# HGRN's state over chunks of 128 tokens, and mLSTM's gate chain in steps between projections

## The chip, the cores and the metric

The kernel runs on one core of one Trainium2 chip. The metric is the device time of one execution in microseconds (us), as the median of the runs given; lower is better.

## The reference, cut to what matters

The program is a two-layer transformer block followed by a second two-layer block. The change touches one stage of the second block, `mixer_ab`: over 256 context and 512 latent tokens it runs HGRN with four heads of 128 x 128 state and mLSTM with four heads, each forward and backward. All of it is float32.

```
def hgrn2_chunk_scan(q, k, v, logf, state0):      # CHUNK = 32
    def step(S, xs):
        b = jnp.cumsum(fc, axis=1)
        b_mid = b[:, CHUNK // 2 - 1:CHUNK // 2]
        b_last = b[:, -1:]
        A = jnp.einsum('bthd,bshd->bhts', qc * jnp.exp(b - b_mid), kc * jnp.exp(b_mid - b))
        A = jnp.where(mask, A, 0.0)
        o = (jnp.einsum('bhts,bshe->bthe', A, vc)
             + jnp.einsum('bthd,bhde->bthe', qc * jnp.exp(b), S))
        S_new = (S * jnp.exp(b_last[:, 0])[..., None]
                 + jnp.einsum('bshd,bshe->bhde', kc * jnp.exp(b_last - b), vc))

def mlstm_chunk_scan(q, k, v, ig, logf, state0):  # its gates alone
        D = jnp.where(mask, bh[..., :, None] - bh[..., None, :] + igh[..., None, :], -jnp.inf)
        m_inter = bh + m[..., None]
        m_t = jnp.maximum(D.max(-1), m_inter)
```

A chunk's tokens act on each other through the matrix A, and on later chunks through the state S. The length of a chunk is free: the decays exp(b) multiply along the tokens, so the same result comes out of longer chunks if A also holds the products between what used to be separate chunks.

## The kernel before

TensorE's order is the order of the code; a scheduler sets the order of the other engines when the kernel is built. All 768 tokens stand side by side in the free dimension. A projection (`proj2`, `mm2`) multiplies one 128-column block of the weights with eight blocks of the normed input; each product of float32 is made of three passes over operands split in two (`hh`/`hl`, `whi`/`wlo`). One of its eight steps is six matmuls on line 1019: three over 512 columns and three over 258. VectorE (DVE) reads the result out of PSUM (`scaled`, L1033 to L1036), ScalarE (ACT) adds biases and splits the weights' high part (L306), GpSimd (POOL) makes the low part in this stage (L307).

Between those steps stands side work. `later` puts a generator at the end of a list, and after each step `tick` advances the first generator of the list by one `yield`. So what a generator issues up to its next `yield` comes on TensorE between two steps of a projection, and if its operands are late, TensorE stands still in front of it, with the projections behind.

`mixer_ab` goes through it in this order:

- the gates' projection and then the whole gate chain of mLSTM (L1088 to L1151): bias, log-sigmoid, two scans over 768 tokens for each direction (L1115, called twice), a running maximum, exponentials, two stores to DRAM (`dm`). `by_token` (L1153 to L1160) transposes two of its results to tokens on partitions; `later` gives it a delay of 16 steps.
- four HGRN heads. `hgrn_in(h)` makes the projections z forward, z backward, q and v, and from z the scan of log decays (L1220), the factors `al`, and the scaled k and q (q by POOL, L1244). `hgrn_core(h)` is a generator with 29 yields: it transposes v to tokens (`tokens`, L1053) and copies it to a block-diagonal `vblk` by four 32-partition copies (L1254), transposes k for both directions, makes A for 128 tokens at a time and keeps the 32 x 32 diagonal blocks by a predicated copy under a mask (L1269, L1271), scales q by `al` on POOL (L1278 to L1281), and then walks through 6 blocks of 128 tokens and 4 chunks of 32 in each. For a block: A times v (L1297), and one product of 512 columns of k with `vblk` that gives the four chunks' state updates side by side (L1302). For a chunk: 32 columns of q times the state (L1313), and the next state by one DVE instruction (L1321), for both directions, then `yield`.
- `conv` and `values` projections, and four mLSTM heads (`mlstm_head`) as generators, the gates' projections, `finish`.

Of the kernel before, what the change touches and what calls it, by code (L numbers as in the profile page):

```python
# [17 lines left out]
P = 128  # L18
# [241 lines left out]
class Body:  # L260
# [800 lines left out]
    def mixer_ab(self, r):  # L1061
# [23 lines left out]
        b = self.small(2)  # L1085
        nc.vector.tensor_scalar(b, ps[:, 0, SC:SC + 2], c2("gb", 0), None, ALU.add)
# [3 lines left out]
        ig, fg = T(), T()  # L1090
        self.both(lambda c, s: nc.vector.tensor_scalar(ig[G, c], tg[G, c], b[G, s:s + 1], None, ALU.add))
        self.both(lambda c, s: nc.vector.tensor_scalar(fg[G, c], tg[H, c], b[H, s:s + 1], None, ALU.add))
        ig, fg = ig[G, :T2], fg[G, :T2]
        ab = T()[G, :T2]
        nc.vector.scalar_tensor_tensor(ab, fg, -1.0, fg, ALU.mult, ALU.max)
        self.log_exp()
        nc.scalar.activation(ab, ab, AF.Exp, scale=-1.0)
        nc.scalar.activation(ab, ab, AF.Ln, bias=self.ones[G, 0:1])
        nc.vector.scalar_tensor_tensor(fg, fg, 0.0, ab, ALU.min, ALU.subtract)
        bc = T()[G, :T2]  # L1100
# [6 lines left out]
        rm, rx = resets(P, 0.0, 1.0), resets(P, -1e30, 0.0)  # L1107
        ch = lambda t, n=P: t.rearrange("p (c n) -> p c n", n=n)

        def scan(out, mask, x, init, op0, op1):  # L1110

            for d in range(2):
                q = slice(32 * d, 32 * d + 32)
                st = (1, -1)[d]
                nc.vector.tensor_tensor_scan(out[q, ::st], mask[q], x[q, ::st], init, op0, op1)  # L1115

        scan(bc, rm, fg, 0.0, ALU.mult, ALU.add)
        aw = T()[:, :T2]
        a = aw[G]
        nc.vector.tensor_tensor(a, ig, bc, ALU.subtract)  # L1120
        cm = T()[G, :T2]
        scan(cm, rx, a, -1e30, ALU.add, ALU.max)

        so = self.ar.tile([P, 12], F32, tag="so", name="so")
        mp = so[:, 6:12]
        nc.vector.tensor_tensor_scan(so[0:32, 0:6], cm[0:32, 127::P], bc[0:32, 127::P], 0.0, ALU.max, ALU.add)
        nc.vector.tensor_tensor_scan(so[32:64, 1::-1], cm[32:64, P::-P], bc[32:64, P::-P], 0.0, ALU.max, ALU.add)
        nc.vector.tensor_tensor_scan(so[32:64, 5:1:-1], cm[32:64, 5 * P:P:-P], bc[32:64, 5 * P:P:-P],
                                     so[32:64, 0:1], ALU.max, ALU.add)
        nc.vector.memset(mp[G], 0.0)  # L1130
        nc.vector.tensor_copy(mp[0:32, 1:6], so[0:32, 0:5])
        nc.vector.tensor_copy(mp[32:64, 0:1], so[32:64, 1:2])
        nc.vector.tensor_copy(mp[32:64, 5:6], so[32:64, 0:1])
        nc.vector.tensor_copy(mp[32:64, 2:5], so[32:64, 3:6])
        mpb = mp[G].unsqueeze(2).to_broadcast([64, 6, P])
        nc.vector.tensor_tensor(ch(cm), ch(cm), mpb, ALU.max)
        dm = self.dr.tile([2, 64, T2], F32, tag="dm", name="dm")
        nc.sync.dma_start(dm[0], cm)
        wi = T()[G, :T2]
        nc.vector.tensor_tensor(ch(wi), mpb, ch(cm), ALU.subtract)  # L1140
        nc.scalar.activation(wi, wi, AF.Exp)
        nc.sync.dma_start(dm[1], wi)
        em = bc
        nc.vector.tensor_tensor(em, bc, cm, ALU.add)
        nc.scalar.activation(em, em, AF.Exp, scale=-1.0)
        wk = T()[G, :T2]
        for n, o in ((0, 127), (32, 0)):
            q = slice(n, n + 32)
            nc.vector.tensor_tensor(ch(wk)[q], ch(a)[q], ch(cm)[q, :, o:o + 1].to_broadcast([32, 6, P]), ALU.subtract)
        nc.scalar.activation(aw[H], wk, AF.Exp)  # L1150
        awc = T()[:, :T2].rearrange("p (t e) -> p t e", e=P)  # L1151
        emc = self.ar.tile([P, 6, 64], F32, tag="emc", name="emc")

        def by_token():
            self.tokens(awc, aw, "v")
            pt = self.aux()
            for t in range(6):
                nc.tensor.transpose(pt[:, t * 64:(t + 1) * 64], em[:, t * P:(t + 1) * P], self.ident[G, 0:64])
            nc.vector.tensor_copy(emc, pt[:, :384].rearrange("p (t e) -> p t e", e=64))
            yield  # L1160

        self.later(by_token(), 16)
# [31 lines left out]
        vblk = self.ar.tile([P, 6, 4, P], F32, tag="vblk", name="vblk")  # L1194
        nc.gpsimd.memset(vblk, 0.0)

        def hgrn_in(h):
            z, zb = [], []
            for d in range(2):
                t = T()  # L1200
                zb.append(self.scaled(t, self.proj2(self.SEG, ("hg", h), d), r))
                z.append(t)
            sg, sn = [], []
# [10 lines left out]
            for d in range(2):  # L1214
# [7 lines left out]
                b3 = ch(bb, 32)  # L1222
# [20 lines left out]
            for d in range(2):  # L1243
                nc.gpsimd.tensor_tensor(res[d][0], res[d][0], q[:, :T2], ALU.mult)  # L1244
# [752 lines left out]
```

## Time and profile before

| what | us |
| --- | --- |
| median of 3 runs (3003.11 to 3011.44) | 3007.16 |
| the profiled execution, its own time | 3008.77 |
| its span in the profile | 3007.0 |
| TensorE (PE) busy | 2888.8 (96%) |
| DVE busy | 1884.5 (63%) |
| ACT busy | 1190.7 (40%) |
| POOL busy | 555.3 (18%) |

The stage of the change lies between 1208 us and about 1695 us of the span. Times in the rows are microseconds from the start of the span unless marked ns. A matmul of full float32 operands shows as two records; those of the projections and transposes show as one. Matmul ends are modelled, so the length of a piece of work on PE is read here from the start of its first record to the start of the next row. A bracket at the end of a row gives the idle time before it and what ended it.

### The profile page before, as it was taken

The numbers are of one execution on the slowest core, as the hardware profiler recorded it, in microseconds if no ns is written. First come the engines' busy times: TensorE is split into PE (matmuls) and PEld (weight loads), VectorE is DVE, ScalarE is ACT, GpSimd is POOL, SyncE is SP. The second block draws the span as 40 slices with busy tenths as digits, with TensorE's granted clock in tenths as the row PEclk, the third lists the DMA queues.
The fourth block names the chain that finished last, engine by engine and source line by source line (L and its number), as shares of the span: only waits on it lengthen the run. The fifth ranks groups of instructions, "written<-read, shape, count | busy, mean of one in ns | idle before, by whom it ended". The sixth has DMA issues, their size and how long they took to land. (4 is left out here: it accounts for less than half of the span.)

```text
span 3007.0 us, 42444 instructions
## 1 busy us (share of the span) xinstructions
PE 2888.8 (96%) x16570; PEld 2466.9 (82%) x16570; DVE 1884.5 (63%) x3608; ACT 1190.7 (40%) x2081; POOL 555.3 (18%) x434
## 2 busy tenths in 40 slices
PE   9999999999999999899999989999999899999997
PEld 7777888877788888766767888888889788899997
DVE  7679995567699976755544563433444779545445
ACT  5663222347542224432334553121123678532223
POOL 3630000046300002423333140000001420300002
PEclk9999999999999999999999999999999999999999
DMA  4235663331266642210121301222222210233332
GB/s 147 69 104 174 200 198 98 89 114 54 70 195 198 197 154 95 69 36 29 36 74 53 106 25 61 63 64 64 64 63 64 78 43 15 95 95 92 96 95 71
DMA packets 98936, 278.47 MB, mean 93 GB/s; under 512 B 11504, under 2 KB 16880, under 8 KB 98224
## 3 DMA queue, kind: packets, MB, share of 16 engines
q1 hardware_dynamic: 98736, 275.76, 29.3%
q8 instruction: 130, 2.13, 0.3%
q14 instruction: 70, 0.57, 0.1%
HBM read 264.84 MB, written 6.68 MB: 90 GB/s over the span
## 5 line engine op out<-in xcount | busy, mean ns | idle before, releaser
L306 ACT ACTIVATE whi<-raw 128x1024 fp32r<-128x1024 f32 (+1 forms) x363 | 377.9, 1042 | 1279.8 <-PE b L1019 468.9
L1019 PE MATMUL b<-hh,whi 128*128 128x512 f32 (+1 forms) x2000 | 655.4, 328 | 0.0
L1019 PE MATMUL b<-hh,wlo 128*128 128x258 f32 x2000 | 475.3, 319 | 0.0
L1019 PE MATMUL b<-hl,whi 128*128 128x512 f32 (+1 forms) x2000 | 469.1, 316 | 0.0
L307 DVE TENSOR_TENSOR wlo<-raw,whi 128x1024 fp32r<-128x1024 f32 (+1 forms) x321 | 391.6, 1220 | 99.1 <-ACT whi L306 97.1
L1019 PEld LDWEIGHTS b<-hh,whi 128*128 128x128 f32 x2000 | 378.9, 189 | 52.5 <-issue 23.1
L1019 PEld LDWEIGHTS b<-hl,whi 128*128 128x128 f32 x2000 | 348.4, 189 | 48.7 <-issue 1.2
L1019 PEld LDWEIGHTS b<-hh,wlo 128*128 128x128 f32 x2000 | 313.9, 191 | 0.0
L334 PE MATMUL b<-hbl,whi 128*128 128x512 f32 x704 | 275.3, 391 | 2.6 <-DVE hbl L345 2.6
L333 PE MATMUL b<-hbh,whi 128*128 128x512 f32 x704 | 275.8, 392 | 1.1 <-ACT hbh L344 1.1
L869 DVE SCALAR_TENSOR_TENSOR junk<-araw,cond 128x512 f32<-128x512 f32 x384 | 271.6, 707 | 7.6 <-ACT cond L355 2.0
L335 PE MATMUL b<-hbh,wlo 128*128 128x512 f32 x704 | 275.1, 391 | 0.2 <-DVE wlo L307 0.2
L1555 POOL TENSOR_TENSOR acc<-acc,t 128x256 f32<-128x256 f32 (+1 forms) x54 | 48.9, 906 | 1011.6 <-ACT t L1550 1010.8
L1019 PE MATMUL b<-t,whi 128*128 128x512 f32 (+1 forms) x864 | 212.5, 354 | 0.0
L392 POOL TENSOR_TENSOR acc<-acc,sq 128x512 f32<-128x512 f32 (+1 forms) x33 | 47.5, 1438 | 761.5 <-ACT sq L389 760.9
L1019 PEld LDWEIGHTS b<-t,whi 128*128 128x128 f32 x864 | 162.3, 188 | 29.8
L334 PEld LDWEIGHTS b<-hbl,whi 128*128 128x128 f32 x704 | 132.8, 189 | 31.4 <-DVE hbl L345 3.3
L333 PEld LDWEIGHTS b<-hbh,whi 128*128 128x128 f32 x704 | 132.7, 189 | 29.5 <-ACT hbh L344 1.5
L335 PEld LDWEIGHTS b<-hbh,wlo 128*128 128x128 f32 x704 | 132.8, 189 | 28.5 <-DVE wlo L307 1.0
L307 POOL TENSOR_TENSOR wlo<-raw,whi 128x1024 fp32r<-128x1024 f32 x42 | 105.7, 2519 | 251.7 <-ACT whi L306 193.0
L335 PE MATMUL b<-hidh,wlo 128*128 128x512 f32 (+1 forms) x352 | 134.1, 381 | 1.1 <-DVE wlo L307 1.1
L333 PE MATMUL b<-hidh,whi 128*128 128x512 f32 (+1 forms) x352 | 133.7, 380 | 0.0
(445 smaller groups left out, 5766.8 us busy)
## 6 DMA issues: line engine op xcount, KB each, us to landing
raw<-w SPq DMA_DIRECT2D x365, 512.0 KB, 3.5
araw<-ada SPq DMA_DIRECT2D x192, 256.0 KB, 3.0
raw<-w SPq DMA_DIRECT2D x18, 256.0 KB, 2.7
xr<-xd SPq DMA_DIRECT2D x2, 2048.0 KB, 8.2
t<-dm SPq DMA_DIRECT2D x8, 384.0 KB, 5.7
x<-xT SPq DMA_DIRECT2D x8, 256.0 KB, 5.2
kTh<-krh SPq DMA_DIRECT2D x32, 64.0 KB, 2.0
kTl<-krl SPq DMA_DIRECT2D x32, 64.0 KB, 2.0
```

What stands on the lines that cost most here:

```text
L306: self.last = nc.scalar.activation(hi[:, :m], r, AF.Copy).ins
L307: self.lo_eng.tensor_tensor(lo[:, :m], r, hi[:, :m].bitcast(F32), ALU.subtract)
L333: t.matmul(out, ah, bh, start=start, stop=False, skip_group_check=True)
L334: t.matmul(out, ah, bl, start=False, stop=False, skip_group_check=True)
L335: t.matmul(out, al, bh, start=False, stop=stop, skip_group_check=True)
L392: nc.gpsimd.tensor_tensor(acc[:, c], acc[:, c], t[:, c], ALU.add)
L869: nc.vector.scalar_tensor_tensor(junk, raw, 1.0, self.cond[:, s, k], ALU.mult, ALU.mult, accum_out=self.adah[:, i, t, s:s + 1])
L1019: t.matmul(ps[:, b, :w_], w[:, s], x[:, o:o + w_], start=(k == 0 and b not in seen), stop=(k == n - 1 and i == 2), skip_group_check=True)
L1555: nc.gpsimd.tensor_tensor(ac, ac, t, ALU.add)
```

## The change

HGRN's state goes over chunks of 128 tokens: six updates for a head and direction in place of 24. The products between the four 32-token chunks of a block, which went through the state before, now go into A in two further levels. At each level k and q are first scaled so that their decays meet at a common point. `hgrn_in` makes 66 decay factors for a direction (`fa`) where it made 24 (`al`).

- Level 1 (L1284 to L1289) makes A as before; DVE then scales half of k (128x12x32).
- Level 2 (L1301 to L1306) multiplies, for each direction, 12 pairs of 32 x 32 tokens, copies them to A with four small DVE copies, scales all of k on DVE (L1305) and all of q on POOL (L1306).
- Level 3 (L1316 to L1323) multiplies 6 pairs of 64 x 64 tokens, copies them to A on ACT, and scales half of k on DVE and half of q on POOL (L1323).
- The transposes of k come after that. The state then takes one product of 128 columns for the update (L1348) and one of all 128 tokens of a block with the state (L1350), and one DVE instruction (L1357), with one `yield` for a block. `vblk`, its memset and its copies are gone.

The gate chain becomes a generator of its own with six yields. `hgrn_in` advances it after the projections z, z and q of heads 1 and 2; what is left would run behind head 2. `by_token` goes to the list behind head 2's core. The arena has 34 tiles in place of 30.

```diff
+        gb = self.small(2)
+        nc.vector.tensor_scalar(gb, ps[:, 0, SC:SC + 2], c2("gb", 0), None, ALU.add)
...
+        def gate_chain():
...
+            ig, fg = T(), T()
+            self.both(lambda c, s: nc.vector.tensor_scalar(ig[G, c], tg[G, c], gb[G, s:s + 1], None, ALU.add))
...
+            nc.vector.scalar_tensor_tensor(ab, fg, -1.0, fg, ALU.mult, ALU.max)
             yield
...
+            self.log_exp()
...
+            scan(bc, rm, fg, 0.0, ALU.mult, ALU.add)
+            yield
...
+            scan(cm, rx, a, -1e30, ALU.add, ALU.max)
+            yield
...
+            nc.sync.dma_start(dm[0], cm)
+            yield
...
+            nc.scalar.activation(em, em, AF.Exp, scale=-1.0)
+            yield
...
+            nc.scalar.activation(aw[H], wk, AF.Exp)
+            yield
...
-        self.later(by_token(), 16)
+            self.later(by_token(), 0)
...
+        chain = gate_chain()
...
-        vblk = self.ar.tile([P, 6, 4, P], F32, tag="vblk", name="vblk")
-        nc.gpsimd.memset(vblk, 0.0)
...
+                if h:
+                    next(chain, None)
...
+                fi, se = (0, 1)[::(1, -1)[d]]
+                b3, b4 = ch(bb, 32), bb.rearrange("p (m i n) -> p m i n", i=2, n=32)
+                fa = self.ar.tile([P, 66], F32, tag="fa", bufs=4, name=self.nm("fa"))
+                lm = self.ar.tile([P, 12, 2], F32, tag="lm", bufs=2, name=self.nm("lm"))
+                f1, gk, hv, dec = fa[:, 0:12], fa[:, 12:24], fa[:, 48:60], fa[:, 60:66]
+                qh = fa[:, 24:48].rearrange("p (m i) -> p m i", i=2)
+                nc.vector.tensor_tensor(lm, b4[:, :, :, last], b4[:, :, :, mid], ALU.subtract)
+                nc.vector.tensor_tensor(f1, lm[:, :, fi], b4[:, :, se, mid], ALU.add)
+                nc.vector.tensor_copy(gk, lm[:, :, se])
+                nc.vector.tensor_copy(qh[:, :, fi], b4[:, :, fi, mid])
+                nc.vector.tensor_tensor(qh[:, :, se], b4[:, :, se, mid], b4[:, :, fi, last], ALU.add)
+                nc.vector.tensor_tensor(hv, b4[:, :, 0, last], b4[:, :, 1, last], ALU.add)
+                nc.vector.tensor_tensor(dec, hv[:, ::2], hv[:, 1::2], ALU.add)
+                nc.scalar.activation(fa, fa, AF.Exp)
...
-            for c in range(4):
-                s = slice(32 * c, 32 * c + 32)
-                nc.vector.tensor_copy(vblk[s, :, c, :], v[s])
...
+                k4 = k.rearrange("p (m i n) -> p m i n", i=2, n=32)[:, :, fi, :]
+                nc.vector.tensor_tensor(k4, k4, fa[:, 0:12].unsqueeze(2).to_broadcast([P, 12, 32]), ALU.mult)
+                yield
+            for d in range(2):
+                q, k, _, fa = res[d]
+                for a, n in ((0, 2), (2, 4)):
+                    ps = self.aux()
+                    pv = ps.rearrange("p (t e) -> p t e", e=P)
+                    for i in range(2):
+                        ko, qo = 64 * i + 32 * d, 64 * i + 32 * (1 - d)
+                        for t in range(n):
+                            o = (a + t) * P
+                            nc.tensor.matmul(pv[ko:ko + 32, t, qo:qo + 32], k[:, o + ko:o + ko + 32], q[:, o + qo:o + qo + 32],
+                                             start=(t == 0), stop=(t == n - 1), skip_group_check=True)
+                        nc.vector.tensor_copy(am[d][ko:ko + 32, a:a + n, qo:qo + 32], pv[ko:ko + 32, 0:n, qo:qo + 32])
+                kh, qb = k.rearrange("p (m n) -> p m n", n=64), ch(q, 32)
+                nc.vector.tensor_tensor(kh, kh, fa[:, 12:24].unsqueeze(2).to_broadcast([P, 12, 64]), ALU.mult)
+                nc.gpsimd.tensor_tensor(qb, qb, fa[:, 24:48].unsqueeze(2).to_broadcast([P, 24, 32]), ALU.mult)
+                yield
+            yield
+            for d in range(2):
+                q, k, _, fa = res[d]
+                ko, qo = 64 * d, 64 * (1 - d)
+                ps = self.aux()
+                pv = ps[:, :384].rearrange("p (t e) -> p t e", e=64)
+                for t in range(6):
+                    nc.tensor.matmul(pv[ko:ko + 64, t, :], k[:, t * P + ko:t * P + ko + 64], q[:, t * P + qo:t * P + qo + 64],
+                                     start=(t == 0), stop=(t == 5), skip_group_check=True)
+                nc.scalar.activation(am[d][ko:ko + 64, :, qo:qo + 64], pv[ko:ko + 64], AF.Copy)
+                hv = fa[:, 48:60].rearrange("p (t i) -> p t i", i=2)
+                for eng, x, i in ((nc.vector, k, d), (nc.gpsimd, q, 1 - d)):
+                    x4 = x.rearrange("p (t i n) -> p t i n", i=2, n=64)[:, :, i, :]
+                    eng.tensor_tensor(x4, x4, hv[:, :, 1 - i].unsqueeze(2).to_broadcast([P, 6, 64]), ALU.mult)
+                yield
+            yield
+            for d in range(2):
+                kt = T()[:, :T2].rearrange("p (t e) -> p t e", e=P)
+                self.tokens(kt, res[d][1], "s")
+                res[d][2] = kt
                 yield
             o = T()[:, :T2].rearrange("p (t e) -> p t e", e=P)
...
-                    pu[d] = self.aux()
-                    c0, c1 = (0, 4) if i < 5 else ((0, 3), (1, 4))[d]
-                    nc.tensor.matmul(pu[d][:, c0 * P:c1 * P], kt[:, t, :], vblk[:, t, c0:c1].rearrange("p c e -> p (c e)"),
-                                     start=True, stop=True)
-                for cc in range(4):
-                    for d in range(2):
-                        q, al = res[d][0], res[d][3]
-                        t = order[d][i]
-                        a = 0 if t < 2 else 2
-                        c = (cc, 3 - cc)[d]
-                        g = t * 4 + c
-                        u = pu[d][:, c * P:(c + 1) * P]
-                        if R[d] is not None:
-                            nc.tensor.matmul(po[d][32 * c:32 * c + 32, (t - a) * P:(t - a + 1) * P],
-                                             q[:, g * 32:(g + 1) * 32], R[d], start=False, stop=False, skip_group_check=True)
-                        if i == 5 and cc == 3:
-                            continue
+                    if i < 5:
+                        pu = self.aux()
+                        nc.tensor.matmul(pu[:, :P], kt[:, t, :], v[:, t, :], start=True, stop=True)
+                    if R[d] is not None:
+                        nc.tensor.matmul(po[d][:, (t - a) * P:(t - a + 1) * P], q[:, t * P:(t + 1) * P], R[d],
+                                         start=False, stop=False, skip_group_check=True)
+                    if i < 5:
...
+                            nc.vector.tensor_copy(nr, pu[:, :P])
                         else:
-                            nc.vector.scalar_tensor_tensor(nr, R[d], st[d], u, ALU.mult, ALU.add)
+                            nc.vector.scalar_tensor_tensor(nr, R[d], fa[:, 60 + t:61 + t], pu[:, :P], ALU.mult, ALU.add)
                         R[d] = nr
-                        st[d] = al[:, g:g + 1]
-                    yield
+                yield
...
+        for _ in chain:
+            pass
...
-        ea = self.arena("ab", 30)
+        ea = self.arena("ab", 34)```

TensorE, the gates' `by_token` (transposes of `t`, L1053 and L1158). Before, in the middle of the v projection of head 0:

```order
L1019 MATMUL b_10883<-hl,whi_10886 128x258
L1019 MATMUL b_10883<-hh,whi_10886 128x258
L1019 MATMUL b_10883<-hh,wlo_10887 128x258
L1019 MATMUL b_10884<-hh,wlo_10887 128x512
L1053 MATMUL b_10897<-cst,t_10669 128x128 x2
L1053 MATMUL b_10901<-cst,t_10669 128x128 x4
L1158 MATMUL b_10907<-cst,t_10660 128x64 x6
L1019 MATMUL b_10884<-hh,whi_10886 128x512
```

After the change, in a `conv` projection, two steps behind the last state product of head 2:

```order
L1019 MATMUL b_12266<-hh,wlo_12270 128x258
L1019 MATMUL b_12267<-hh,wlo_12270 128x512
L1053 MATMUL b_12304<-cst,t_11160 128x128 x2
L1053 MATMUL b_12308<-cst,t_11160 128x128 x4
L1170 MATMUL b_12314<-cst,t_11037 128x64 x6
L1019 MATMUL b_12267<-hh,whi_12269 128x512
```

It moved from the 17th step behind the gates' projection to about the 108th; the first head's v is transposed at the same step as before.

TensorE, the third of the six blocks of a head (`t` are k, q, A or v as tiles, `hR` the state). Before, the block's first yield and the step behind it, which come with three more of the L1313 pairs in this block:

```order
L1297 MATMUL b_11425<-t_11209,t_10701 128x128 x4
L1302 MATMUL b_11430<-vblk,t_11230 128x512
L1297 MATMUL b_11432<-t_11209,t_10702 128x128 x4
L1302 MATMUL b_11437<-vblk,t_11247 128x512
L1313 MATMUL b_11425<-hR_11412,t_10790 32x128
L1313 MATMUL b_11432<-hR_11415,t_10804 32x128
L1019 MATMUL b_11346<-hh,whi_11348 128x512
```

After the change, the whole of the block:

```order
L1343 MATMUL b_11417<-t_11182,t_10655 128x128 x4
L1348 MATMUL b_11422<-t_11182,t_11344 128x128
L1350 MATMUL b_11417<-hR_11402,t_10742 128x128
L1343 MATMUL b_11427<-t_11182,t_10656 128x128 x4
L1348 MATMUL b_11432<-t_11182,t_11361 128x128
L1350 MATMUL b_11427<-hR_11407,t_10760 128x128
L1019 MATMUL b_11325<-hh,whi_11327 128x512
```

The update's product went from 512 columns to 128, and the four pairs of 32-token products became one pair of 128-token products.

DVE after the change, in the first head: between the first predicated copy of level 1 and the scaling of k that level 2 waits for (L1289) the scheduler has put the gate chain's second scan (L1123) and factors of the next head:

```order
L1286 COPY_PREDICATED t_10655<-msk,b_11199 128x256
L1123 SCALAR_TENSOR_TENSOR t_11162<-t_11041,t_11160 32x768 x2
L1244 TENSOR_TENSOR fa_11065<-lm_11066,t_11063 128x12
L1245 COPY fa_11065<-lm_11066 128x12
L1246 COPY fa_11083<-t_11081 128x12
L1249 TENSOR_TENSOR fa_11065<-fa_11065 128x6
L1247 TENSOR_TENSOR fa_11083<-t_11081 128x12
L1248 TENSOR_TENSOR fa_11083<-t_11081 128x12
L1286 COPY_PREDICATED t_10655<-msk,b_11203 128x512
L1289 TENSOR_TENSOR t_10727<-t_10727,fa_10744 128x12x32
```

Before, the whole chain stood in one piece ahead of the read-out of the next projection (L1033); its last rows and that read-out:

```order
L1136 TENSOR_TENSOR t_10671<-t_10671,so 64x768
L1140 TENSOR_TENSOR t_10686<-so,t_10671 64x768
L1144 TENSOR_TENSOR t_10660<-t_10660,t_10671 64x768
L1149 TENSOR_TENSOR t_10692<-t_10669,t_10671 32x768 x2
L1033 TENSOR_TENSOR t_10707<-b_10372,acc_7155 128x256
```

The chain's instructions went from one closed piece to places behind the read-outs of the projections of heads 1 and 2, among those heads' own work.

## Rows read from the trace of the kernel before

**Rows 1.** The page's first part: engines' busy time, share, instructions.

```profile
PE 2888.8 (96%) x16570; PEld 2466.9 (82%) x16570; DVE 1884.5 (63%) x3608; ACT 1190.7 (40%) x2081; POOL 555.3 (18%) x434
```

**Rows 2.** Busy time by stretches of 20 us inside the stage.

```profile
core 0: us, PE busy (x) PEld busy (x) DVE busy (x) ACT busy (x) POOL busy (x), PEclk, DMA share, GB/s
1220.00:1240.00 20.00, 9.97 (x52) 8.27 (x51) 17.82 (x26) 7.00 (x10) 6.88 (x6) 0.77 0.24 62
...
1300.00:1320.00 20.00, 20.00 (x120) 12.95 (x120) 7.67 (x26) 1.45 (x2) 2.39 (x1) 1.00 0.12 41
...
1620.00:1640.00 20.00, 19.05 (x83) 13.67 (x82) 10.56 (x26) 9.51 (x23) 2.36 (x1) 0.75 0.09 27
```

**Rows 3.** PE's waits in the stage, 1208 to 1700 us: total, times, longest.

```profile
PE b L1053 <- DVE sml L1036: 10.0, 1, 10.0
```

**Rows 4.** PE in order of time around the gates' `by_token`: start, length, instruction.

```profile
1236.56 1.51 PE L1053 MATMUL b<-cst,t 128*128 128x128 f32 x6 [10.03 <-DVE sml L1036]
...
1238.84 0.79 PE L1019 MATMUL b<-hh,whi 128*128 128x512 f32 x1
...
1240.93 0.40 PE L1019 MATMUL b<-hh,whi 128*128 128x512 f32 x1
```

**Rows 5.** DVE in order of time, the gate chain up to the first read-out.

```profile
1226.16 3.52 DVE L1115 TENSOR_TENSOR_SCAN t<-t,t 32x768 f32<-32x768 f32 x2
...
1235.39 0.42 DVE L1033 TENSOR_TENSOR t<-b,acc 128x256 f32<-128x256 f32 x1
```

**Rows 6.** PE in order of time: heads' first and following rows, two steps of the third.

```profile
1273.99 0.82 PE L1053 MATMUL b<-cst,t 128*128 128x128 f32 x6
...
1338.67 0.50 PE L1019 MATMUL b<-hh,whi 128*128 128x512 f32 x1
...
1340.87 0.82 PE L1053 MATMUL b<-cst,t 128*128 128x128 f32 x6
...
1408.79 0.50 PE L1019 MATMUL b<-hh,whi 128*128 128x512 f32 x1
...
1409.96 0.40 PE L1019 MATMUL b<-hh,whi 128*128 128x512 f32 x1
...
1411.02 0.82 PE L1053 MATMUL b<-cst,t 128*128 128x128 f32 x6
...
1468.61 0.50 PE L1019 MATMUL b<-hh,whi 128*128 128x512 f32 x1
...
1469.85 0.41 PE L1313 MATMUL b<-hR,t 128*32 128x128 f32 x4
1470.19 0.50 PE L1019 MATMUL b<-hh,whi 128*128 128x512 f32 x1
...
1490.78 0.44 PE L1053 MATMUL b<-cst,t 128*128 128x128 f32 x2 [1.16 <-ACT t L1045]
1491.52 0.66 PE L1053 MATMUL b<-cst,t 128*128 128x128 f32 x4 [0.30 <-ACT t L1045]
...
1550.86 0.50 PE L1019 MATMUL b<-hh,whi 128*128 128x512 f32 x1
```

**Rows 7.** PE in order of time: full float32 products of 128 and of 512 columns.

```profile
1279.14 1.50 PE L1269 MATMUL b<-t,t 128*128 128x128 f32 x12
1280.39 0.48 PE L1019 MATMUL b<-hh,whi 128*128 128x512 f32 x1
...
1307.10 1.02 PE L1302 MATMUL b<-vblk,t 128*128 128x512 f32 x2
1307.96 1.05 PE L1297 MATMUL b<-t,t 128*128 128x128 f32 x8
```

**Rows 8.** PE, another stage: products with 64-row outputs, 128 columns.

```profile
124.04 2.13 PE L679 MATMUL b<-wsp,t 128*64 128x128 f32 x28
```

**Rows 9.** DVE's 128x768 product beside POOL's work, and alone.

```profile
1356.93 2.57 DVE L1470 TENSOR_TENSOR t<-t,sml 128x768 f32<-128x768 f32 x1
...
1685.72 0.96 DVE L1470 TENSOR_TENSOR t<-t,sml 128x768 f32<-128x768 f32 x1 [0.93 <-ACT sml L1469]
```

**Rows 10.** POOL's scaling of q (L1278): least, median, longest in ns, first and last start.

```profile
L1278 POOL TENSOR_TENSOR t<-t,al x4: 1429/1588/2142, 1285.9 to 1498.8; 128x736 f32<-128x736 f32 x4
```

More of the change, by code (lines that the diff above doesn't have):

```diff
@@ L1089, in mixer_ab @@
         nc.vector.tensor_tensor(tg[:, SC:T2], ps[:, 1, :], r[:, SC:T2], ALU.mult)
[L1090 to L1100, printed above, removed]
+        ch = lambda t, n=P: t.rearrange("p (c n) -> p c n", n=n)
         def resets(n, v0, v1):
@@ L1105, in resets @@
             return m
-        rm, rx = resets(P, 0.0, 1.0), resets(P, -1e30, 0.0)
-        ch = lambda t, n=P: t.rearrange("p (c n) -> p c n", n=n)
-        def scan(out, mask, x, init, op0, op1):
-            for d in range(2):
[L1113 to L1136, printed above, removed]
-        dm = self.dr.tile([2, 64, T2], F32, tag="dm", name="dm")
-        nc.sync.dma_start(dm[0], cm)
@@ L1139, in mixer_ab @@
[L1139 to L1149, printed above, removed]
@@ L1150, in mixer_ab @@
-        nc.scalar.activation(aw[H], wk, AF.Exp)
-        awc = T()[:, :T2].rearrange("p (t e) -> p t e", e=P)
[L1152 to L1159, printed above, removed]
-            yield
@@ L1221, in hgrn_in @@
                 mid, last = ((15, 31), (16, 0))[d]
-                b3 = ch(bb, 32)
-                al = self.ar.tile([P, 24], F32, tag="al", bufs=4, name=self.nm("al"))
-                lm = self.ar.tile([P, 24], F32, tag="lm", bufs=2, name=self.nm("lm"))
-                nc.vector.tensor_tensor(lm, b3[:, :, last], b3[:, :, mid], ALU.subtract)
-                nc.vector.tensor_copy(al, lm)
-                if d == 0:
-                    nc.vector.tensor_tensor(al[:, 0:23], lm[:, 0:23], b3[:, 1:24, mid], ALU.add)
-                else:
-                    nc.vector.tensor_tensor(al[:, 1:24], lm[:, 1:24], b3[:, 0:23, mid], ALU.add)
-                    nc.vector.tensor_tensor(al[:, 0:1], lm[:, 0:1], b3[:, 23:24, mid], ALU.add)
-                nc.scalar.activation(al, al, AF.Exp)
+                fi, se = (0, 1)[::(1, -1)[d]]
[12 more added lines that the diff above has]
+                nc.scalar.activation(fa, fa, AF.Exp)
                 bm = f
@@ L1239, in hgrn_in @@
                 nc.vector.scalar_tensor_tensor(kk, kk, omlb[:, d, h:h + 1], bm, ALU.mult, ALU.mult)
-                res.append([e1, kk, None, al])
+                res.append([e1, kk, None, fa])
             q = T()
             self.addb(q, self.scaled(q, self.proj2(self.SEG, ("hg", h), 2), r))
+            if h:
+                next(chain, None)
             for d in range(2):
@@ L1251, in hgrn_core @@
             self.tokens(v, vf, "s")
-            for c in range(4):
-                s = slice(32 * c, 32 * c + 32)
-                nc.vector.tensor_copy(vblk[s, :, c, :], v[s])
             yield
-            for d in range(2):
-                kt = T()[:, :T2].rearrange("p (t e) -> p t e", e=P)
-                self.tokens(kt, res[d][1], "s")
-                res[d][2] = kt
-                yield
             am = []
             for d in range(2):
-                q, k, kt, al = res[d]
+                q, k, _, fa = res[d]
+                fi = d
                 m = amask[d][:, :T2].rearrange("p (t e) -> p t e", e=P)
+                am.append(m)
                 for a, n in ((0, 2), (2, 4)):
@@ new lines, in hgrn_core @@
+            yield
+            for d in range(2):
+                q, k, _, fa = res[d]
+                ko, qo = 64 * d, 64 * (1 - d)
+                ps = self.aux()
+                pv = ps[:, :384].rearrange("p (t e) -> p t e", e=64)
+                for t in range(6):
+                    nc.tensor.matmul(pv[ko:ko + 64, t, :], k[:, t * P + ko:t * P + ko + 64], q[:, t * P + qo:t * P + qo + 64],
[6 more added lines that the diff above has]
+                yield
@@ L1282, in hgrn_core @@
+            yield
+            for d in range(2):
+                kt = T()[:, :T2].rearrange("p (t e) -> p t e", e=P)
+                self.tokens(kt, res[d][1], "s")
+                res[d][2] = kt
                 yield
@@ L1907, in second @@
         eb.close()
-        ea = self.arena("ab", 30)
+        ea = self.arena("ab", 34)
         self.lo_eng = nc.gpsimd
```

65 lines of the change are left out of this document (49 added, 16 removed).

## The prediction

> **What bounds the kernel now.** The page's first part says TensorE: PE is busy for 96% of the span, no other engine for more than 63% [rows 1]. So a time counts only if PE gets shorter or waits less, and the place to look is the stage of the change. The view by stretches shows both kinds there [rows 2]: between 1300 and 1320 us PE has no gap at a full clock and DVE is busy for 7.67 of 20 us, while between 1220 and 1240 us PE works for 9.97 of 20 us and DVE for 17.82. PE's waits name the reason [rows 3]: one wait of 10.0 us in front of L1053, put down to DVE. In order of time, that L1053 is the gates' `by_token`, which needs the end of the gate chain [rows 4]; DVE runs the chain in one piece, with a pair of scans of 3.52 us, and reads out the next projection only at 1235.39 [rows 5]. For the HGRN heads I read PE in order of time at each head's first row and at the row behind it [rows 6], and the price of each kind of product from runs of equal records [rows 7, 8].
>
> **Gate chain.** It adds and removes no work of weight. It goes from one piece into six, so DVE reads out projections in between, and `by_token` comes some 90 steps later, when its operands are old. What goes is the wait of 10.03 us and the slow clock behind it: `by_token` and the step after it take 2.28 us and 2.09 us [rows 4], and an undisturbed step takes 1.06 us (1409.96 to 1411.02 [rows 6]), half of 2.09. So 1.03 us of the step and 1.14 us of `by_token` go as well: **12.2 us** together. The chain's DVE work is hidden by DVE's free time, 12 of 20 us between 1300 and 1320 [rows 2]. Its two stores to `dm` stand five and seven weight loads later on SP's queue; a store that waits for the running maximum holds the loads queued behind it, but those are issued ahead of their projections, and the readers of `dm` are the mLSTM heads, after all four HGRN heads. I cost the stores at nothing. If that cover fails, a projection waits for its weights.
>
> **State, what is removed.** In the third head, which has no wait, PE takes 59.17 us (1411.02 to 1470.19 [rows 6]); 28 steps of projections of 1.06 us lie in it, 29.7 us, so the side work is 29.5 us. A product of 512 columns takes 0.86 us (1307.10 to 1307.96 [rows 7]). A head has ten and two of 384 columns (three quarters, 0.64 us): 9.9 us. A pair of 32-token state products takes 0.34 us and makes the step ahead of it 1.24 us long in place of 1.06 (1468.61, 1469.85, 1470.19 [rows 6]), 0.52 us; 23 pairs give 12.0 us. Together 21.9 us. A product of 128 columns takes 0.21 us (12 records, two for a product, from 1279.14 to 1280.39 [rows 7]); the new state has ten for the update and ten for the output, 4.2 us. Saved for a head: 17.7 us.
>
> **State, what is added on PE.** Level 2 has 12 products, 24 records, for a direction; level 3 has 6 products, 12 records. No row of before has outputs of 32 rows by 32 columns. A record of 128 columns costs 0.104 us [rows 7]; if columns alone count, 32 cost a quarter, 0.026, and 64 cost 0.052; if they don't count, 0.104. The nearest row is L679, 64-row outputs, 28 records in 2.13 us, 0.076 [rows 8], with 128 columns. I take 0.05 for level 2 and 0.065 for level 3, which lie between a share by columns and that row: 2 x 24 x 0.05 + 2 x 12 x 0.065 = 4.0 us (ends 2.5 and 7.5). A head now breaks into the projections 15 times; at 0.1 us a time, between nothing and the 0.18 us beside narrow products [rows 6], less what the transposes and A cost in this way before, that is 1.2 us. So a head saves 17.7 - 4.0 - 1.2 = 12.5 us (ends 14 and 9), four heads **50 us** (56 to 36). The Trainium skill speaks against many small products: on its page "TensorE: Matmul & The Clock Gate", section "Step-by-step: what each phase is for", the sequencer spends about 62 ns on each matmul where the hardware decoder is off. By that, the 72 records of a head would be an estimated 4.5 us, and four heads would save 2 us less; no row here shows a record so small.
>
> **What is added beside PE.** On DVE a head loses 44 state updates and the four `vblk` copies, and gets eight updates, eight copies out of PSUM and six scalings of k. The scalings stand between levels: level 2 waits for level 1's copies and L1289, level 3 for L1305 on DVE and L1306 on POOL, the transposes for L1323. POOL scaled q in 1.43 to 2.14 us [rows 10]; it now does so in full and then by half. There is room: from level 2 to level 3 of one direction lie three steps and the other direction's level 2, 3 x 1.06 + 1.2 = 4.4 us, and from a state update to its use a step and some 0.6 us. DVE and ACT work for the factors is as long as before to within some small instructions.
>
> **Waits that come and go.** Before, the first, second and fourth head take 64.68, 67.92 and 60.08 us against 59.17 [rows 6]: 15.2 us of waits and slow clock. I expect the same places to be late again, and others. First head: by the DVE order the chain's second scan, 3.52 us [rows 5], and some 2.5 us of copies and factors stand in front of L1289, and PE brings 1.25 + 2 x 1.06 = 3.4 us of cover: about 2.5 us late; the rest of the piece in front of L1305 gives as much again: 5 us. Second head: chain pieces between state updates, 3 us. Third: v is transposed one step behind its own projection. The fourth head waits 1.16 + 0.30 us for v with three steps of room [rows 6]; two steps less make 3.6 us. Fourth: 1.5 us as before. With two stretches of slow clock, priced as behind the gate chain at about 2 us each, 17 us. So this term is **-2 us** (from +15, no wait at all, to -20).
>
> **Sum.** 12 + 50 - 2 = 60 us. The profiled execution took 3008.8 us and would take 2948.8; the median of the runs shown lies 1.6 us under it, so 2947 us.
>
> **Rivals.**
>
> *DVE and POOL hold each other up.* Behind level 2 DVE scales k and POOL scales q, at the same moment by construction. A DVE product of 128x768 took 2.57 us beside POOL's work and 0.96 alone [rows 9]. If each of the eight L1305 is longer by 1.6 us, each half-size L1323 by 0.8, and all of it reaches PE, that is 19 us: 2966 us. Against it: the 4.4 us of room cover 0.6 us of copies and 2.57. The Trainium skill has this as a rule, "SBUF — State Buffer", section "SBUF: two separate sides": the two engines share a pair of ports as an exclusive lock, and the loser stands for the whole instruction. By that rule every one of these pairs collides; the rows agree.
>
> *No new waits.* DVE is lighter, every piece fits: the 17 us don't come, 2930 us. For it: DVE's free time [rows 2]. Against it: the scheduler's DVE order in the first head.
>
> *The gate chain's wait comes back* (the change doesn't do what it says): `by_token` or a head catches the chain's tail in one piece, 12 us: 2959 us. Against it: about 90 steps of room.
>
> *The clock stays at its lower level through the heads*, and the kernel gets slower. Between 1620 and 1640 us the mean granted clock was 0.75 with PE busy for 19.05 us [rows 2]: short waits are enough for it. A changed head is 17 us of side work and 17 steps of 1.06 us, 35 us; four heads 140 us. At 1.2 GHz all the way they take 140 us more: 3087 us. It decides from 60 of the 140 us at the lower level on. Against it: before, with a wait possible at each of 46 updates of a head, the third and fourth heads run at full clock.
>
> **How the numbers follow.** Forecast 2947 us, chance 0.55; DVE and POOL 0.2; no new waits 0.15; the chain's wait 0.07; the slow clock 0.03. The forecast's own ends are 56 and 36 us for the products and a few us for waits; with the rivals at 2930 and 2966 and these ends, 2918 to 2978 us leaves out about 2 in 10. Faster by over 0.3% (9 us, about what a measurement of this kernel can tell from no change) is every case but the last, and a bad sum of price ends and waits: 0.95; within 0.3%: 0.02; slower: 0.03.
>
> **What would show it.** Right: no PE wait near 10 us behind the gates' projection, no step of 2.1 us there; an undisturbed head some 35 us long in place of 59, with 17 steps in it; level 2 at about 1.2 us and level 3 at about 0.8 us for a direction; PE's waits of the heads in front of levels 2 and 3 of the first head and of the third head's v. Wrong: level 2 near 2.5 us; waits behind L1305 or L1306 in every head; the granted clock under 0.9 through the heads.

## The result, and the profile after

The changed kernel takes 2980.7 us (median of 4 runs, 2978.8 to 2982.5) against 3005.9 us in the same comparison: a ratio of 0.9914, 95% interval 0.9897 to 0.9931, or 25 us less. The forecast was 60 us less. The profiled execution took 2982.45 us, its span 2980.2. From the gates' projection to the output projection the stage went from 486.5 to 454.3 us, 32 us less; in later stages, where TensorE's order is the same, this execution gave back 5 us. Those 5 us are the clock's: the same stretch of PE's work, some 3800 records, takes 621.5 us before (from 1952.8 us, mean granted clock 0.99) and 627.4 us after (from 1921.0 us, 0.98), and in the run "cores two steps later", below, again 621.5 us at 0.99.

The page's first part, as [rows 1]:

```profile
PE 2845.4 (95%) x16554; PEld 2479.1 (83%) x16554; DVE 1874.6 (63%) x3532; ACT 1192.8 (40%) x2085; POOL 560.6 (19%) x437
```

PE is 43 us less busy and the kernel only some 26 us shorter: work has become waiting. The view by stretches, columns as in [rows 2], shows where:

```profile
1260.00:1280.00 20.00, 8.40 (x66) 7.43 (x66) 19.62 (x36) 7.32 (x13) 7.88 (x3) 0.80 0.09 26
1300.00:1320.00 20.00, 20.00 (x148) 18.70 (x146) 8.58 (x20) 4.11 (x8) 3.85 (x2) 1.00 0.16 52
1340.00:1360.00 20.00, 11.37 (x69) 10.11 (x69) 16.91 (x36) 12.08 (x20) 7.23 (x3) 0.91 0.09 27
```

Inside the first and second head PE stands for about half the time while DVE is nearly full; between them there is room. PE's waits in the stage, as [rows 3]:

```profile
PE b L1301 <- DVE t L1303: 15.8, 16, 5.0
PE b L1301 <- DVE fa L1244: 6.6, 1, 6.6
PE b L1348 <- ACT t L1059: 5.7, 2, 4.3
PE b L1053 <- ACT t L1045: 4.7, 4, 3.3
PE b L1455 <- issue: 3.6, 1, 3.6
PE b L1350 <- DVE hR L1357: 3.3, 2, 1.8
```

The wait of 10.0 us behind the gates' projection is gone. In its place stands one that occurs 16 times, four in each head, between level 2's products (L1301) and level 2's copies (L1303). The third head in order of time, PE; a direction of level 2 is 24 records:

```profile
1371.86 0.44 PE L1053 MATMUL b<-cst,t 128*128 128x128 f32 x2 [0.69 <-ACT t L1045]
...
1379.09 0.31 PE L1301 MATMUL b<-t,t 128*32 128x32 f32 x4
1379.70 0.45 PE L1301 MATMUL b<-t,t 128*32 128x32 f32 x12 [0.30 <-DVE t L1303]
1380.63 0.44 PE L1301 MATMUL b<-t,t 128*32 128x32 f32 x8 [0.48 <-DVE t L1303]
1381.00 0.50 PE L1019 MATMUL b<-hh,whi 128*128 128x512 f32 x1
...
1382.25 0.31 PE L1301 MATMUL b<-t,t 128*32 128x32 f32 x4
1383.82 0.45 PE L1301 MATMUL b<-t,t 128*32 128x32 f32 x12 [1.25 <-DVE t L1303]
1384.77 0.64 PE L1301 MATMUL b<-t,t 128*32 128x32 f32 x8 [0.49 <-DVE t L1303]
1385.33 0.80 PE L1019 MATMUL b<-hh,whi 128*128 128x512 f32 x1
...
1411.58 0.48 PE L1019 MATMUL b<-hh,whi 128*128 128x512 f32 x1
```

and DVE beside it:

```profile
1381.43 2.08 DVE L1305 TENSOR_TENSOR t<-t,fa 128x768 f32<-128x768 f32 x1
1383.55 0.22 DVE L1303 COPY t<-b 32x64 f32<-32x64 f32 x1
```

The two halves of a buffer are written one behind the other, with a DVE copy of the first between them, and the second half's first product waits for that copy. PE stands twice in each direction. In the second direction the copy is itself late: the first direction's scaling of k, L1305, is ahead of it on DVE. The program's order shows the wait as a semaphore on DVE at the second half's first product:

```
L1301 MATMUL b_11233<-t_10742,t_10727 32x32 [waits DVE_49,Activation_49]
L1301 MATMUL b_11233<-t_10742,t_10727 32x32
L1301 MATMUL b_11233<-t_10742,t_10727 32x32 [waits DVE_49]
L1301 MATMUL b_11233<-t_10742,t_10727 32x32
```

In the first head the same waits meet a DVE that works on the gate chain and the next head's factors. PE, then DVE, then POOL:

```profile
1274.45 0.39 PE L1301 MATMUL b<-t,t 128*32 128x32 f32 x4 [6.61 <-DVE fa L1244]
1279.84 0.65 PE L1301 MATMUL b<-t,t 128*32 128x32 f32 x12 [4.99 <-DVE t L1303]
1282.09 0.64 PE L1301 MATMUL b<-t,t 128*32 128x32 f32 x8 [1.60 <-DVE t L1303]
```

```profile
1269.10 3.52 DVE L1123 TENSOR_TENSOR_SCAN t<-t,t 32x768 f32<-32x768 f32 x2
...
1272.74 0.17 DVE L1245 COPY fa<-lm 128x12 f32<-128x12 f32 x1
...
1273.77 0.54 DVE L1289 TENSOR_TENSOR t<-t,fa 128x384 f32<-128x384 f32 x1
...
1274.32 1.81 DVE L1245 COPY fa<-lm 128x12 f32<-128x12 f32 x1
...
1278.65 1.01 DVE L1257 SCALAR_TENSOR_TENSOR t<-t,lb,t 128x768 f32<-128x768 f32 x1
1279.58 0.20 DVE L1303 COPY t<-b 32x64 f32<-32x64 f32 x1
```

```profile
1273.84 4.03 POOL L1264 TENSOR_TENSOR t<-t,t 128x768 f32<-128x768 f32 x2 [8.03 <-ACT t L1254]
```

Before 1274.45 the wait is put down to a small addition, L1244; ahead of L1289 on DVE stand the chain's scan of 3.52 us and the next head's factors. With the chain moved away ("chain beside the conv projections", below) 3.5 of these 6.6 us remain. The copy L1303, 0.20 us of work, came 5 us behind its products.

### The profile page after: what moved, and what is told of

It reads as the page before. It is cut to its first block, busy times and chain, and to the rows that moved or that the text cites. A ratio compares the mean times of both kernels' runs of the same rounds, so it can differ in the third digit from the quotient of the medians.

```text
span 2980.2 us, 42310 instructions
## 1 busy us (share of the span) xinstructions
PE 2845.4 (95%) x16554; PEld 2479.1 (83%) x16554; DVE 1874.6 (63%) x3532; ACT 1192.8 (40%) x2085; POOL 560.6 (19%) x437
## 3 DMA queue, kind: packets, MB, share of 16 engines
q8 instruction: 130, 2.13, 0.3%
## 5 line engine op out<-in xcount | busy, mean ns | idle before, releaser
L1019 PE MATMUL b<-hh,whi 128*128 128x512 f32 (+1 forms) x2000 | 649.3, 325 | 0.0
L1019 PE MATMUL b<-hh,wlo 128*128 128x258 f32 x2000 | 476.2, 320 | 0.0
L1019 PE MATMUL b<-hl,whi 128*128 128x512 f32 (+1 forms) x2000 | 470.5, 317 | 0.0
L307 DVE TENSOR_TENSOR wlo<-raw,whi 128x1024 fp32r<-128x1024 f32 (+1 forms) x321 | 391.7, 1220 | 102.4 <-ACT whi L306 100.6
L1019 PEld LDWEIGHTS b<-hh,whi 128*128 128x128 f32 x2000 | 379.9, 190 | 33.5 <-issue 4.0
L1019 PEld LDWEIGHTS b<-hl,whi 128*128 128x128 f32 x2000 | 349.4, 189 | 50.5 <-issue 0.2
L1019 PEld LDWEIGHTS b<-hh,wlo 128*128 128x128 f32 x2000 | 314.5, 191 | 0.0
L1019 PE MATMUL b<-t,whi 128*128 128x512 f32 (+1 forms) x864 | 212.5, 354 | 0.0
L1019 PEld LDWEIGHTS b<-t,whi 128*128 128x128 f32 x864 | 162.3, 188 | 29.7
L307 POOL TENSOR_TENSOR wlo<-raw,whi 128x1024 fp32r<-128x1024 f32 x42 | 107.4, 2559 | 188.3 <-ACT whi L306 182.8
```

The source lines that it names most:

```text
L307: self.lo_eng.tensor_tensor(lo[:, :m], r, hi[:, :m].bitcast(F32), ALU.subtract)
L1019: t.matmul(ps[:, b, :w_], w[:, s], x[:, o:o + w_], start=(k == 0 and b not in seen), stop=(k == n - 1 and i == 2), skip_group_check=True)
```

## The experiments

Theory A holds two losses apart: level 2 waits for copies out of its own buffer, and the chain's pieces stand on DVE where the first two heads need it. Lengths of the heads, from the first transposes of v to the row behind the last state product, in us (before: [rows 6]):

| kernel | head 0 | 1 | 2 | 3 | median us | ratio to before, interval |
| --- | --- | --- | --- | --- | --- | --- |
| before | 64.7 | 67.9 | 59.2 | 60.1 | 3005.9 | |
| the change | 52.0 | 49.2 | 39.7 | 37.8 | 2980.7 | 0.9914 (0.9897 to 0.9931) |
| chain alone | 71.9 | 66.4 | 59.5 | 63.0 | 2999.8 | 0.9981 (0.9971 to 0.9990) |
| state alone | 46.1 | 42.5 | 38.2 | 40.5 | 2978.6 | 0.9914 (0.9902 to 0.9927) |
| copies last | 45.8 | 47.2 | 34.8 | 34.5 | 2957.9 | 0.9843 (0.9829 to 0.9858) |
| chain beside conv | 45.8 | 44.2 | 39.8 | 36.3 | 2966.2 | 0.9874 (0.9859 to 0.9890) |
| both | 39.9 | 38.5 | 34.7 | 32.8 | 2946.8 | 0.9809 (0.9795 to 0.9823) |
| own buffers | 46.3 | 46.4 | 34.8 | 34.0 | 2963.9 | 0.9872 (0.9851 to 0.9892) |
| copies last, chain whole | 39.9 | 42.7 | 34.7 | 35.3 | 2959.5 | 0.9856 (0.9835 to 0.9876) |

The kernels were measured in four comparisons, each beside its own runs of the kernel before (medians 3001.4 to 3005.9 us). So a difference of medians between two rows can be some us off, and the ratios are the better measure.

**Chain alone.** The kernel before, with `gate_chain`, its `next` calls and `by_token` from the change.

> The kernel before with the gate chain alone in six steps (same six places, by_token behind head 2's core); HGRN's state as before. Theory A (the chain's pieces hurt where they stand: DVE works on them while TensorE stands in front of the first two heads' products): the 12.2 us behind the gates' projection come, heads 0 and 1 give back 4 to 9 us: 2996 to 3002 us by the profiled time of 3008.8 us, 2993 to 2999 by the median. Theory B (the pieces are harmless, what was lost is lost inside the new levels): all 12 us and by_token's 1.3 us stay, 2991 to 2994 by the median.

Measured: 5 us less, 2999.8 us. Head 0 is 7 us longer than before, the four heads together 9 us, of the 13.5 us that were gained in front of them. This is theory A's account, with a median just above its 2993 to 2999 us; theory B falls.

**State alone.** The change with the chain in one piece:

```diff
-            self.later(by_token(), 0)
+            self.later(by_token(), 16)
         chain = gate_chain()
+        for _ in chain:
+            pass
```

> The changed kernel with the gate chain in one piece, as before; the new state alone. Theory A: the wait of 10 us and the slow clock behind it come back (12 to 13.5 us), but head 0, 52 us long in the changed kernel, falls to about 38 and head 1 from 49 to about 43: 2972 to 2978 us by the median, faster than the changed kernel. Theory B: heads 0 and 1 stay as long as they are, the kernel is 12 to 14 us slower than the changed one: 2993 to 2995 us.

Measured: 2978.6 us, not to be told from the change. Heads 0 and 1 are 5.9 and 6.7 us shorter, 12.6 together, and a wait of 8.1 us behind the gates' projection is back. So in the places that the change gives it, the stepped chain is worth nothing. Theory A had the heads' direction, but too much: the two heads stay at 46 and 43 us, 4 to 8 us over the third's 38.2, with no piece of the chain in them, and the kernel is no faster than the changed one.

**Copies last.**

```diff
-                        nc.vector.tensor_copy(am[d][ko:ko + 32, a:a + n, qo:qo + 32], pv[ko:ko + 32, 0:n, qo:qo + 32])
+                    for ko, qo in ((32 * d, 32 - 32 * d), (64 + 32 * d, 96 - 32 * d)): nc.vector.tensor_copy(am[d][ko:ko + 32, a:a + n, qo:qo + 32], pv[ko:ko + 32, 0:n, qo:qo + 32])
```

> The changed kernel, where level 2 issues the copy of a buffer's first half behind the products of its second half, so no product waits for a copy out of its own buffer. Theory A: level 2 of an undisturbed direction falls from 1.9 and 2.9 us to about 1.1 us, 2.5 us a head and up to 5 us more in head 0: 2966 to 2971 us. Theory C (DVE's queue is what is late, L1305 in front of the next copies above all; the handoff only shows it): the time moves to the waits in front of level 3 and of A times v, and the kernel stays within 2978 to 2983 us.

Measured: 2957.9 us, 23 us less than the change and more than I expected. The third head:

```profile
1361.30 0.44 PE L1053 MATMUL b<-cst,t 128*128 128x128 f32 x2 [0.69 <-ACT t L1045]
...
1368.52 0.72 PE L1301 MATMUL b<-t,t 128*32 128x32 f32 x24
1369.17 0.50 PE L1019 MATMUL b<-hh,whi 128*128 128x512 f32 x1
...
1370.41 0.72 PE L1301 MATMUL b<-t,t 128*32 128x32 f32 x24
...
1373.36 0.91 PE L1316 MATMUL b<-t,t 128*64 128x64 f32 x12
1374.20 0.50 PE L1019 MATMUL b<-hh,whi 128*128 128x512 f32 x1
...
1396.06 0.48 PE L1019 MATMUL b<-hh,whi 128*128 128x512 f32 x1
```

The same 24 records run without a gap, in 0.65 us to the next row in place of 1.9 and 3.1, and the head takes 34.8 us. The stage is 434.9 us long in place of 454.3. Theory C falls: only 2.2 us came back in front of level 3 (L1316), in head 0.

**Chain beside the conv projections.** `next(chain)` behind conv 1 to 3 and in head 3's `hgrn_in`, `by_token` ahead of head 3's core, which starts without its delay of 2 steps:

```diff
-                if h:
+                if h == 3:
...
         for j in range(4):
             conv(j)
+            if j:
+                next(chain, None)
-        self.later(hgrn_core(3, *hgrn_in(3)), 2)
+        last = hgrn_in(3)
+        for _ in chain:
+            pass
+        self.later(hgrn_core(3, *last), 0)
```

> The changed kernel with the chain's six pieces behind the conv projections 1 to 3 and head 3's projections z, z and q, by_token in front of head 3's core: heads 0 and 1 see no piece of it. Theory A: head 0 falls from 52 to about 38 us, head 1 from 49 to about 43 us, and the pieces fit beside 48 steps with no side work: 2960 to 2966 us. Theory D (it is the next head's own factors and POOL's multiplications of q, which slow DVE, that are late in heads 0 and 1): both heads stay over 46 us, 2976 to 2983 us.

Measured: 2966.2 us, 14.5 less than the change, heads 0 and 1 shorter by 6.1 and 5.0 us. By the ratios it is 12 us less, in the stage 12.9 (441.4 us). Near theory A in the time, but the heads stay at 46 and 44 us, over its 38 and 43: a part of D seems to hold too, the next head's work on DVE and POOL. The rows for it are under the next run.

**Both edits.**

> The changed kernel with both edits, level 2's copies last and the chain beside the conv projections. Theory A (two separate losses): the gains of the two, 22.8 and 14.5 us, add up but for what head 0 counts twice (its wait for its own copies, some 6 us, went in both): 2946 to 2953 us. Rival (both only made DVE's late work in head 0 shorter, the same loss twice): 2955 to 2958 us.

Measured: 2946.8 us; the losses are separate: in the stage the two edits take off 19.4 and 12.9 us alone, 33.0 us together (421.3 us). This version beats both kernels. What PE still waits for in its stage:

```profile
PE b L1301 <- DVE t L1289: 4.8, 2, 3.5
PE b L1455 <- issue: 3.6, 1, 3.6
PE b L1348 <- ACT t L1059: 3.5, 2, 2.1
PE b L1053 <- ACT t L1163: 2.5, 1, 2.5
```

The first of these lies in head 0, where no piece of the chain is left. PE, DVE and POOL there:

```profile
1268.38 0.72 PE L1301 MATMUL b<-t,t 128*32 128x32 f32 x24 [3.51 <-DVE t L1289]
```

```profile
1266.53 1.80 DVE L1289 TENSOR_TENSOR t<-t,fa 128x384 f32<-128x384 f32 x1
1268.25 1.79 DVE L1249 TENSOR_TENSOR fa<-fa 128x6 f32<-128x6 f32 x1
```

```profile
1266.10 3.92 POOL L1264 TENSOR_TENSOR t<-t,t 128x768 f32<-128x768 f32 x2 [3.27 <-ACT t L1254]
```

While POOL multiplies the next head's q (L1264), L1289 takes 1.80 us in place of 0.54, and a product of 128x6 elements as long. So some 1.3 of the 3.5 us are DVE and POOL holding each other up, as theory D has it; the next head's factors stand on DVE ahead of that. The wait in front of L1455, which the profile puts down to nothing, is of the same kind. That product reads `W`, which DVE's L1436 makes, and in the changed kernel it starts right behind the second of three L1436. Ahead of these stand on DVE, and beside them on POOL:

```profile
1518.25 3.11 DVE L1405 SCALAR_TENSOR_TENSOR t<-t,t 128x768 f32<-128x768 f32 x1
1521.28 1.81 DVE L1404 COPY sml<-t 128x6 f32<-128x6 f32 x1
1523.13 0.96 DVE L1405 SCALAR_TENSOR_TENSOR t<-t,t 128x768 f32<-128x768 f32 x1
```

```profile
1518.15 2.39 POOL L307 TENSOR_TENSOR wlo<-raw,whi 128x1024 fp32r<-128x1024 f32 x1
1520.49 2.53 POOL L1385 TENSOR_TENSOR t<-madd,t 128x768 f32<-128x768 f32 x1
```

The first two take 3.8 us more than a L1405 (0.96 us, the third row) and a small copy (0.17) took with POOL idle, and PE waits 3.6 us. No run moves POOL's work here, so the rows show the collision and its length, and not what taking it away would gain.

**Cores two steps later**, on top of both (delays of 2 in place of 0).

> The kernel with both edits, and the cores of heads 1, 2 and 3 start two steps later, so v is transposed three steps behind its projection. If v's read-out is what the three heads wait for at their start (0.7 and 0.4 us in head 2, up to 3.3 and 0.4 us in head 3, a slow step behind each): 3 to 5 us less than with both edits. If the bulk is whatever DVE and ACT still have to do there: within 1.5 us of it.

Measured: 2945.8 us, ratio 0.9800 (0.9786 to 0.9814): no difference. The waits for v are gone (heads 2 and 3 take 33.3 and 33.0 us), but others grew: head 1 has one of 2.7 us in front of its first update product (L1348), and in `mlstm_head` that in front of L1455 is 4.1 us in place of 3.6, with a new one of 2.3 us later on (L1458). So the second of the two expectations holds.

**q scaled by DVE behind level 2**, on top of both:

```diff
-                nc.gpsimd.tensor_tensor(qb, qb, fa[:, 24:48].unsqueeze(2).to_broadcast([P, 24, 32]), ALU.mult)
+                nc.vector.tensor_tensor(qb, qb, fa[:, 24:48].unsqueeze(2).to_broadcast([P, 24, 32]), ALU.mult)
```

> The kernel with both edits, where DVE scales q behind level 2 (L1306) in place of POOL. Rival of my prediction (DVE and POOL hold each other up): L1305 falls from 1.6 to 2.1 us to 0.96 us each where nothing of POOL runs beside it, DVE's two products together take about what L1305 took beside POOL's, and the time stays within 2 us. If POOL is not what lengthens L1305, it stays at 1.6 us or more, L1306 comes on top with 1 us or more, and level 3 waits: 4 to 8 us slower.

Measured: 2950.6 us, ratio 0.9814 (0.9801 to 0.9828). The third head with both edits, DVE and POOL, then DVE with q on it, and PE's new wait:

```profile
1354.81 1.71 DVE L1305 TENSOR_TENSOR t<-t,fa 128x768 f32<-128x768 f32 x1
...
1357.64 1.03 DVE L1305 TENSOR_TENSOR t<-t,fa 128x768 f32<-128x768 f32 x1
```

```profile
1354.22 1.48 POOL L1306 TENSOR_TENSOR t<-t,fa 128x768 f32<-128x768 f32 x1 [6.54 <-PE b L1301]
```

```profile
1356.82 0.96 DVE L1305 TENSOR_TENSOR t<-t,fa 128x768 f32<-128x768 f32 x1
1357.69 0.95 DVE L1306 TENSOR_TENSOR t<-t,fa 128x768 f32<-128x768 f32 x1
```

```profile
PE b L1316 <- DVE t L1306: 5.9, 4, 1.6
```

POOL's scaling does lengthen L1305 where it starts first: from 0.96 to 1.71 us in the first direction, to 1.03 in the second. The first agrees with the Trainium skill, "SBUF — State Buffer", section "SBUF: two separate sides", by which the engine that starts second stands until the other's instruction is over: POOL's ends at 1355.70, L1305 0.82 us behind it. But DVE's two products take 1.9 us together, level 3 now waits for the second of them four times, and the median moves by 3.8 us the wrong way, inside the intervals. So the collision is real, and giving POOL's part to DVE gains nothing. It was tried only with the copies last. In the changed kernel L1305, 2.08 us long, stands ahead of the second direction's copy, and the product behind that waits 1.25 us against 0.30 in the first direction: nearly 1 us a head of the handoff's loss is the collision's, an estimate from these rows.

**k's transposes copied by DVE**, on top of the later cores.

> The kernel with both edits and the later cores, and k's transposes are copied out by DVE in place of ACT. If the wait of 1.4 to 4.3 us in front of the first update products of heads 1 and 2 is ACT's queue (a table load and the next head's logarithms ahead of the copies): it goes, 3 to 6 us less than with the later cores alone. If DVE is as late there: no change, or slower by up to 4 us.

Measured: 2949.4 us, ratio 0.9805 (0.9786 to 0.9824): no gain. The wait in front of L1348 in head 1, 2.7 us with the later cores, is now one of 3.9 us for DVE's copy, L1057.

**Copies last, chain whole.** The edits of "state alone" and "copies last" together.

> The changed kernel with level 2's copies last and the gate chain in one piece, as before: what the chain's steps are worth once level 2 doesn't wait for its own copies. If the pieces cost heads 0 and 1 as much as the gates' stall did (as in the kernel with the handoff, where one piece or six gave the same time): 2956 to 2960 us, the time of level 2's copies last alone. If the pieces were dear only because each wait in level 2 met a DVE that worked on them, one piece is now dearer by the stall's 12 us less some 4 us: 2964 to 2969 us.

Measured: 2959.5 us, as copies last with the chain in steps. Where the steps stand decides: beside the heads they gain nothing, beside conv 12.7 us (2946.8; 14 by the ratios).

**Own buffers.** Each half takes a buffer of its own, the copies stay between the products:

```diff
-                    ps = self.aux()
-                    pv = ps.rearrange("p (t e) -> p t e", e=P)
                     for i in range(2):
+                        pv = self.aux().rearrange("p (t e) -> p t e", e=P)
```

> The changed kernel, where each half of a level-2 buffer gets a PSUM buffer of its own and the copies stay where they are, between the products. If what holds TensorE is that a product waits for a copy out of its own buffer: the same gain as with the copies last, 2955 to 2962 us. If it is where the copies stand in DVE's order, whatever buffer they read: no gain, 2978 to 2983 us. Four buffers for a direction in place of two may make a product wait for an older buffer: up to 5 us of it back.

Measured: 2963.9 us, 17 less than the change (13 by the ratios, 17.3 in the stage). Of the 16 waits one is left (line 1302 is the copy here):

```profile
PE b L1300 <- DVE t L1302: 2.3, 1, 2.3
```

So it is the shared buffer that makes the product wait, not the place of the copies. The wait that is left is in head 0, for an older buffer, which is the price named beforehand.

## Why the prediction was wrong

*Gate chain, 12.2 us: right as a size, wrong as a gain.* From the start of the gates' projection to head 0's first row it is 13.5 us less, of which `by_token`, 1.3 us, only moved. But the same DVE work cost heads 0 and 1 12.6 us (the change against state alone). I had allowed 8 us for them. I had the chain's work "hidden by DVE's free time", and read that free time between 1300 and 1320 us; but the pieces from 1264 us on landed inside the heads, and between 1260 and 1280 us DVE was busy for 19.62 of 20 us. To cost the two stores at nothing was right: they waited on SP's queue for 16.9 and 19.9 us, and no projection waited for its weights.

*State, removed and added: right, a little low.* A head was to take 35 us; with the copies last, heads 2 and 3 take 34.8 and 34.5. That nearness is in part luck, for the first of them holds 2.5 us of waits. In the run with later cores, where next to none is left, they take 33.3 and 33.0. Such a head holds 16 steps of projections (96 records of L1019), not 17, so its side work is about 16.0 us in place of 29.5: 13.5 us saved, where I had 12.5, and some 54 us for four heads (an estimate from these rows). Level 3 measured 0.84 us for a direction (forecast 0.8). Level 2's products alone are cheaper than priced: 0.65 us in place of 1.2. The Trainium skill ("TensorE: Matmul & The Clock Gate", "Step-by-step: what each phase is for") states about 62 ns for a matmul where the hardware decoder is off. That is not what these rows show: 24 records in 0.65 us are 27 ns each.

*What failed: "Waits that come and go", -2 us.* The stage became 32 us shorter; with 12.2 us from the gates and 54 from the state, this term came to about -34. I wrote that the "scalings stand between levels" and looked for waits there alone. Inside level 2 the program itself hands a buffer from PE to DVE and back, twice a direction. That was to be read from the diff: a copy in the loop over `i`, out of a buffer that is made outside it. It costs 23 us by the median, 21 by the ratios (0.9914 less 0.9843 of 3005 us), 19.4 in the stage. The 16 waits themselves are 15.8 us; the rest is mostly the clock, for over the four heads PE is busy for 208.9 us at a mean granted clock of 0.93, and for 204.0 us at 0.95 with the copies last. Over the 35 us of an undisturbed head, the four heads lost 17, 14, 5 and 3 us, 39 in all; I had 17 with the slow clock. The chain's pieces are the second loss, 12 us by the ratios. The two together, 33 us, and the 5 us of the clock in later stages, less the 4 us that the state saved above its forecast, are about the 35 us that were missing. That both edits together end at the forecast's 2947 us is in part chance: their stage is 65 us shorter where I had 60, and 4 us are lost in later stages.

*Rivals.* DVE and POOL: the mechanism is there. At L1305, where I had put it, an instruction is longer by 1.1 us and not 1.6, and about 1 us a head of that reaches PE; where PE does wait for it, in front of level 2 of the first head and of L1455, I had not looked. No new waits: wrong. The chain's wait coming back: not as a wait at `by_token`, but the 12 us did, in the heads. The slow clock: the granted clock was 0.80 and 0.91 in the two bad stretches and 1.00 between them, 0.93 over the four heads; the kernel didn't get slower.

Open: what the waits in front of L1301 in head 0 and in front of L1455 would be with POOL's work elsewhere, and the second head's remaining 4 to 6 us over the third's.

## What to carry to other kernels

When a step is split into small products, list for each product the buffer it writes and who reads that buffer next; a copy between two products of one buffer is a full round trip between engines, which cost more here than all the products of its level. Issue all products of a buffer, then its copies. Work that is given out in steps to fill gaps must be put beside steps in which its engine has nothing due: the same chain was worth 0 us in one place and 13 in another.

## What the hardware showed that was not expected

Products of 32 rows by 32 columns took 27 ns a record (24 in 0.65 us), against 104 ns for 128 columns [rows 7]: about by their columns. Those of 64 by 64 took 70 ns (12 in 0.84 us), more than half of 104. A DVE copy of 128x12 elements took 0.17 us at 1272.74 and 1.81 us at 1274.32, where POOL's L1264 ran beside it: a small instruction was held up for longer, by 1.6 us, than L1305 on 128x768 elements, by 1.1 us.
